# A fourth tile for weight first parts (and, for a while, remainders) in the first mixer, constants fetched one by one, and output tiles stored by another queue

## The chip, the cores and the metric

The kernel runs on one core of a Trainium2 chip. The core has five engines with queues of their own: TensorE (PE, matrix products; its weight loads are listed apart as PEld), VectorE (DVE), ScalarE (ACT), GpSimd (POOL) and SyncE (SP, which here only issues DMAs). Each works through its own list of instructions in order and waits at semaphores for the others. The metric is the time of one execution on the device in microseconds (us), as the median of several runs.

## What is computed

Two layers of a decoder trunk on x of 256 rows (time) by 2048 columns, all in float32. The first layer has a mixer of two parallel halves, the second an attention mixer; each is followed by a gated feed-forward with a causal convolution. Only the first mixer and the very end of the last feed-forward matter here:

```python
def mixer_ab(h, w_in, sp_w, sp_b, v_gain, lower_bound, o_gain, w_out):
    u, v, q, f, i, g = jnp.split(h @ w_in, cuts, axis=-1)        # each 256 x 1024
    u = gelu(u); v = rms_norm(gelu(v) per head) * v_gain
    mixed = einsum('hts,bcshd->bcthd', tril(sp_w), v) + sp_b     # chunks of 128 rows
    y_a = u * mixed
    y_b = hgrn2(q, f, i, g, lower_bound, o_gain)                 # 8 heads, gated recurrence
    return concatenate([y_a, y_b], -1) @ w_out

x = x + mixer_ab(rms_norm(x), ...)
x = x + conv_ffn(rms_norm(x), ...)
x = x + mixer_c(rms_norm(x), ...)
x = x + conv_ffn(rms_norm(x), ...)
```

## The kernel before

x lies transposed on chip: 16 tiles of 128 columns by 256 rows (xT[0] to xT[15]), kept in seven larger tiles of 1, 1, 2, 2, 2, 4 and 4 of them (x0, x1, x2, x4, x6, x8, x12 in the lists of instructions). Every weight is streamed through once, in **pieces** of 128 x 1024 numbers (512 KB): 128 in the first mixer, 816 in the kernel (a few are rounded in two halves).

float32 accuracy comes from two rounded parts. For each piece, SyncE loads `w` (L196), ScalarE rounds it to the first part `wh` (L183), VectorE subtracts to get the remainder `wl` (L184). TensorE then multiplies three times, activations likewise being split: wh with the first part, wl with the first part, wh with the remainder (L357 to L359 in `project_four`, L338 to L340 in `project_tok`, L314 in `project`). The tiles come from `three` (L169): 5 buffers of w, 3 of wh and 3 of wl in the first mixer; the tile of piece n is that of piece n-3, so its rounding must wait until TensorE is through with piece n-3. `weights` (L194) ties the loads, roundings and subtractions to the order of the pieces.

Everything else is fitted between the pieces. Its work is written as Python generators that lie in `queue` and `flight`; `tick()` (L133), called once for each piece, lets each of up to depth[0] generators go on to its next `yield`. A generator thus hands out its instructions some pieces later, and a yield more or less moves what follows by a piece. `held(r, "wl")` puts an instruction behind the last wl handed out, `early` ahead of the one three pieces on, `tied` behind the last matmul. Within these ties a scheduler sets each engine's final order, by its own simulated times and by when buffers come free.

The first mixer's program order: `project_first` for v (w_v), while the norm's sums of squares are made; then `fetch_late` (L536) four times, which issues on ScalarE's queue the loads of the spatial weights `spw` and `spb` into the two tiles `wt`, of the remaining columns of the parameters `pp`, and of the masks `kst`; then, piece by piece, w_f (2 groups of 8 pieces, `gates`), the 8 heads' w_q with w_i between them (`values`, `flip`, `hgrn`), w_g (`gated`), w_u (`spatial`) and the output projection w_abo (`add_four`). Beside the pieces of w_f and the first of w_q runs `mixes` (L581): gelu on v, its sums of squares, the normalisation of gv in four multiplications (L606), and the spatial product (L570, L572). `hgrn(h)` (L686 on) is the recurrence of one head; `gated(j)` multiplies its normalised output (L793) by silu of the gate (L827).

`add_four(q, ...)` (L476) takes a quarter of the output projection (4 column tiles): ScalarE copies it (L478), VectorE transposes it in two halves (L370), 16 transfers of 32 KB by SyncE and GpSimd (L377) set the blocks in place in `dst`, and some pieces later VectorE adds them to x (L490); each x tile is split again for the feed-forward's first matmuls (ScalarE L385, VectorE L389) and its squares are summed (L452, L456). The quarter q=3 is added while the first pieces of the feed-forward's w_up are already under way.

At the end, the last feed-forward adds three quarters of its output in the same manner (`add_y`, L1298), the last quarter tile by tile straight from the sums (L1331), and `finish_x` (L1310) stores each finished tile: the last four tiles (m 12 to 15) one by one (L1314), the others when their larger tile is complete (L1316), all on SyncE.

Of the kernel before, what the change touches and what calls it, by code (L numbers as in the profile page):

```python
# [15 lines left out]
P = 128  # L16
# [39 lines left out]
def tile_trunk(ctx: ExitStack, tc: tile.TileContext, x, pp_d, cst_d, mlev_d, msk_d,  # L56
# [98 lines left out]

    deep = {"pool": None, "turn": 0, "dma": None}

# [11 lines left out]
    def three(n):  # L169
# [10 lines left out]
        return w, wh, wl  # L180

    def halves(w, wh, wl):
        r = deep["wh"] = SC.activation(wh, w, AF.Copy)  # L183
        deep["wl"] = V.tensor_tensor(wl, w, wh.bitcast(F32), ALU.subtract)  # L184
        return r
# [8 lines left out]
    def weights(src, n, rows=None):  # L194
        w, wh, wl = three(n)
        in_order("w", nc.sync.dma_start(w if rows is None else w.rearrange("p (m c) -> p m c", m=rows), src))  # L196
        halves(w, wh, wl)
        for what in ("wh", "wl"):
            in_order(what, deep[what])
        pieces[0] += 1  # L200
        for n_, what, r in list(ahead):
            if n_ <= pieces[0]:
                tc.add_manual_dep(deep[what].ins, r.ins.name, order, reason="before")
                ahead.remove((n_, what, r))
        return wh, wl
# [296 lines left out]
    def mixer_ab(norm):  # L502
# [21 lines left out]
        for g, ps in enumerate(project_first(w_v, norm, lambda: queue.append(finish()))):  # L524
# [5 lines left out]
            else:  # L530
                drain()
                Rt = norm.Rt
                last = ps
        A = norm.a

        def fetch_late(*args, behind="wh"):  # L536
            r = SC.dma_start(*args)
            tc.add_manual_dep(r.ins, deep[behind].ins.name, order, reason="queue order")
# [5 lines left out]

        wt = [wide("wt").rearrange("p (h c) -> p h c", h=NH) for _ in range(2)]
        fetch_late(wt[0], spw_d)
        fetch_late(wt[1], spb_d.partition_broadcast(P))
        fetch_late(pp[:, C_CW:NPP], pp_d[:, C_CW:NPP])
        msk = hp.tile([P, NL * P], U16, tag="msk", name="msk")
        kst = hp.tile([P, NL - 1, 2, P], F32, tag="E", name="kst", bufs=2).rearrange("p a b c -> p (a b c)")[:, 0:NL * P]  # L550
        fetch_late(kst, msk_d)
        near, tri = kst[:, (NL - 1) * P:NL * P], cst[:, K_TRI:K_TRI + P]
# [28 lines left out]
        def mixes():  # L581
# [19 lines left out]
            for g in range(2):  # L601
                yield
                for T in range(2):
                    i = (2 * g + T) * 4
                    v4 = gv[g][:, T].rearrange("p (h d) -> p h d", d=P)
                    held(V.tensor_tensor(v4, v4, ss[:, i:i + 4].unsqueeze(2).to_broadcast([P, 4, P]),  # L606
                                         ALU.mult), "wl")
# [4 lines left out]
            for h in range(0, NH, 2):  # L612
                ps = bank()
                both = [mix(h + i, ps[:, i * S:(i + 1) * S]) for i in range(2)]
                for m in both:
                    next(m)
                for m in both:
                    next(m, None)
                yield


# [7 lines left out]
        def bound():  # L629
# [10 lines left out]
            V.tensor_scalar(lb, lb, 2.0 ** -63, None, ALU.max)  # L640

        queue.append(mixes())
        lf, kq = [], []

# [41 lines left out]
        def hgrn(h):  # L686
# [29 lines left out]
            waiting.append(diagonal)  # L716
            yield
            if waiting:
# [7 lines left out]
            for li in reversed(range(NL)):  # L726
# [12 lines left out]
                if 1 < n < 64:  # L739
                    yield  # L740
            for _ in range(2):
                yield
# [55 lines left out]
        def flip(itok, late):  # L798
            tmp, rows = (hp.tile([P, 512], F32, tag="ar", name=nm(n), bufs=3) for n in ("tmp", "rows"))
            V.transpose(tmp, late)  # L800
            V.transpose(rows.rearrange("p (c j) -> p c j", j=BLK), view(tmp, BLK - 1, (BLK, P // 8), (-1, BLK)))
            yield
            for b in range(4):
                nc.gpsimd.dma_start(itok[BLK * b:BLK * (b + 1), 1], rows[BLK * (3 - b):BLK * (4 - b)])
            yield
            itoks.append((itok, steps[0]))

        def values(j):
            ps = project_tok(w_i[j], norm)
            itok = hp.tile([P, 2, 512], F32, tag="tok", name=nm("itok"), bufs=2)  # L810
            late = hp.tile([P, 512], F32, tag="ar", name=nm("late"), bufs=3)
            SC.activation(cols2(late), of_two(ps[1]), AF.Copy, scale=Rt[:, 1:2])
# [30 lines left out]
        for h in range(NH):  # L843
# [7 lines left out]
            for T in range(2):  # L851
                q = kq[h][:, 2 - T]
                SC.activation(back(q) if T else q, view(ps, T, (2, P)), AF.Copy, scale=omlb[:, h:h + 1])
            queue.append(hgrn(h))
        for j in range(2):
            ps = project_four(w_g[4 * j:4 * j + 4], A, KT)
# [38 lines left out]
        for q in range(4):  # L895
# [12 lines left out]
            if q == 0:  # L908
                depth[0] = 2
            add_four(q, ps, z, tmp, dst, nxt, 2 if q in (1, 2) else 1, (nc.sync, nc.gpsimd) if q else (nc.gpsimd,))  # L910
        es.close()
        banks(ctx, 4)
# [304 lines left out]
    def ffn(l, norm, last):  # L1217
# [69 lines left out]
        def add_y(q, finish):  # L1287
# [5 lines left out]
            def rest():  # L1293
                for _ in range(3 if near else LAG - 2 * (q == 3)):
                    yield
                for i in range(4):
                    m = 4 * q + i
                    held(V.tensor_tensor(xT[m], xT[m], zt[:, i], ALU.add), "wl")  # L1298
                    if finish:
                        finish_x(m)  # L1300
                    if not near and (q < 3 or i % 2):
                        yield
# [7 lines left out]
        def finish_x(m):  # L1310
            if last:
                t, i, end = part[m]
                if m >= KT - 4:
                    nc.sync.dma_start(out[:, m, :], xT[m])  # L1314
                elif m == end:
                    nc.sync.dma_start(out[:, m - i:m + 1, :], t)  # L1316
            else:
                nxt.feed(m)
# [127 lines left out]
```

## Time and profile before

| | us |
|---|---|
| median of 3 runs | 2169.62 (2169.5, 2169.62, 2169.9) |
| the profiled execution | 2170.91 |
| its span, first to last instruction | 2169.1 |
| first mixer within it | 0 to about 387 |
| first feed-forward | about 387 to 1058 |
| second mixer, second feed-forward | about 1058 to 1506, to 2169 |

The spans are from one profiled execution on the one core, with a mean granted TensorE clock of 1.000. Durations in the text are from its trace; a matmul's listed length (0.38 us) is longer than the distance to the next one's start, as matmuls overlap, so distances between starts are what counts. In rows of the trace, `out<-in` are tiles by the program's names, and the bracket at the end gives the time for which the engine sat idle before the instruction and what ended it. The lists of instructions further down come from the compiled programs: they show order, not time.

### The profile page before, as it was taken

What the parts mean: (1) busy time and instruction counts of PE and PEld (TensorE: products, weight loads), DVE (VectorE), ACT (ScalarE), POOL (GpSimd) and SP (SyncE); (2) the same over time, 40 slices, a digit from 0 to 9 for tenths busy, and PEclk for the clock granted to TensorE, in tenths of its full rate; (3) what the DMA queues carried; (4) which work ended last, traced back from release to release, by engine and by line L of the source; (5) the groups of instructions that cost most, each with busy time, mean ns of one, the idle gap of its engine ahead of it and who ended that gap; (6) DMA issues with size and microseconds to landing.
All of it is one profiled execution on the core that took longest, in us unless ns stands there. A gap on an engine that the chain in (4) does not pass through costs nothing.

```text
span 2169.1 us, 32427 instructions
## 1 busy us (share of the span) xinstructions
PE 2162.7 (100%) x10874; PEld 1900.2 (88%) x10874; DVE 1616.6 (75%) x2258; ACT 1322.6 (61%) x1951; POOL 458.9 (21%) x841
## 2 busy tenths in 40 slices
PE   9999999999999999999999999999999999999999
PEld 8898888888888888888888888888888888888888
DVE  7788768777567757876987787877787577667766
ACT  7688756666556546664565556766666466456642
POOL 0242231212012002111133443221211012012102
PEclk9999999999999999999999999999999999999999
DMA  8665777877676767776777767777777677767766
GB/s 307 204 183 183 217 227 229 247 228 231 214 222 206 241 206 221 242 216 208 245 229 226 241 206 212 227 239 222 240 243 214 200 235 218 228 213 225 235 209 189
DMA packets 492871, 484.06 MB, mean 223 GB/s; under 512 B 115264, under 2 KB 460496, under 8 KB 492576
## 3 DMA queue, kind: packets, MB, share of 16 engines
q1 hardware_dynamic: 465888, 453.27, 66.6%
q0 software_dynamic: 25088, 26.44, 5.3%
q10 hardware_dynamic: 1728, 2.28, 0.4%
q8 instruction: 85, 1.39, 0.3%
q14 instruction: 82, 0.67, 0.1%
HBM read 435.18 MB, written 2.11 MB: 202 GB/s over the span
## 4 chain that ended last, share of the span: by engine, by line
PE 96%; DVE 1%; DMA 1%; ACT 1%; issue 0%; SPq 0%; DVEq 0%; ACTq 0%
PE pm L358 26%; PE pm L357 26%; PE pm L359 26%; PE pm L338 5%; PE pm L340 4%; PE pm L339 4%; PE pm L314 3%; DVE wl L184 1%; DMA w<-in_w_f 1%; PE pm L246 0%; ACT wh L183 0%; DMA w<-in_w_v 0%; PE pm L270 0%; PE px L1040 0%; PE px L1094 0%
## 5 line engine op out<-in xcount | busy, mean ns | idle before, releaser
L184 DVE TENSOR_TENSOR wl<-w,wh 128x1024 fp32r<-128x1024 f32 (+1 forms) x820 | 994.7, 1218 | 453.1 <-ACT wh L183 439.2
L183 ACT ACTIVATE wh<-w 128x1024 fp32r<-128x1024 f32 (+1 forms) x820 | 859.2, 1051 | 640.7 <-PE pm L359 492.8
L358 PE MATMUL pm<-wl,a 128*128 128x512 f32 x1728 | 655.2, 379 | 1.0 <-DVE wl L184 0.9
L357 PE MATMUL pm<-wh,a 128*128 128x512 f32 x1728 | 655.9, 380 | 0.0
L359 PE MATMUL pm<-wh,a 128*128 128x512 f32 x1728 | 654.9, 379 | 0.0
L377 POOL DMA_DIRECT2D zt<-tmp x413 | 224.3, 551 | 1134.0 <-DVE tmp L370 1020.8
L358 PEld LDWEIGHTS pm<-wl,a 128*128 128x128 f32 x1728 | 326.6, 189 | 48.0 <-DVE wl L184 2.2
L359 PEld LDWEIGHTS pm<-wh,a 128*128 128x128 f32 x1728 | 326.6, 189 | 46.2
L357 PEld LDWEIGHTS pm<-wh,a 128*128 128x128 f32 x1728 | 326.5, 189 | 46.2
L357 PE MATMUL pm<-wh,hid 128*128 128x512 f32 x688 | 260.8, 379 | 0.0
L358 PE MATMUL pm<-wl,hid 128*128 128x512 f32 x688 | 260.8, 379 | 0.0
L359 PE MATMUL pm<-wh,hid 128*128 128x512 f32 x688 | 260.8, 379 | 0.0
L338 PE MATMUL pm<-wh,a 128*128 128x512 f32 x448 | 170.8, 381 | 0.0
L340 PE MATMUL pm<-wh,a 128*128 128x512 f32 x448 | 169.9, 379 | 0.0
L339 PE MATMUL pm<-wl,a 128*128 128x512 f32 x448 | 169.8, 379 | 0.0
L358 PEld LDWEIGHTS pm<-wl,hid 128*128 128x128 f32 x688 | 130.0, 189 | 18.5
L359 PEld LDWEIGHTS pm<-wh,hid 128*128 128x128 f32 x688 | 130.0, 189 | 18.5
L357 PEld LDWEIGHTS pm<-wh,hid 128*128 128x128 f32 x688 | 130.0, 189 | 18.4
L377 POOL DMA_DIRECT2D turn<-tmp x160 | 87.2, 553 | 226.0 <-DVE tmp L370 128.4
L1252 ACT ACTIVATE conv<-zt,pp 128x256 f32<-128x256 f32 x176 | 103.4, 589 | 46.5 <-DMA zt<-tmp 31.9
L370 DVE STREAM_TRANSPOSE tmp<-z 128x512 f32<-128x512 f32 x120 | 100.9, 858 | 9.3 <-ACT z L1238 6.8
L1253 DVE SCALAR_TENSOR_TENSOR conv<-zt,pp,conv 128x255 f32<-128x255 f32 x176 | 84.1, 478 | 30.7 <-ACT conv L1252 25.8
(244 smaller groups left out, 2202.4 us busy)
## 6 DMA issues: line engine op xcount, KB each, us to landing
w<-in_w_up SPq DMA_DIRECT2D x352, 512.0 KB, 5.1
w<-in_w_dn SPq DMA_DIRECT2D x176, 512.0 KB, 5.0
w<-in_w_cqkv SPq DMA_DIRECT2D x96, 512.0 KB, 5.0
w<-in_w_abo SPq DMA_DIRECT2D x32, 512.0 KB, 5.0
w<-in_w_cg SPq DMA_DIRECT2D x32, 512.0 KB, 5.3
w<-in_w_co SPq DMA_DIRECT2D x32, 512.0 KB, 5.1
zt<-tmp SPq DMA_DIRECT2D x414, 32.0 KB, 2.2
zt<-tmp POOLq DMA_DIRECT2D x413, 32.0 KB, 2.0
```

What stands on the lines that cost most here:

```text
L183: r = deep["wh"] = SC.activation(wh, w, AF.Copy)
L184: deep["wl"] = V.tensor_tensor(wl, w, wh.bitcast(F32), ALU.subtract)
L338: PE.matmul(to_two(ps[T]), ah, h, start=k + i == 0, stop=False)
L339: PE.matmul(to_two(ps[T]), ah, l, start=False, stop=False)
L340: deep["last"] = PE.matmul(to_two(ps[T]), al, h, start=False, stop=k + i == KT - 1)
L357: PE.matmul(to_rows(ps[T]), ah, h, start=not begun and k + i == ks[0], stop=False)
L358: PE.matmul(to_rows(ps[T]), ah, l, start=False, stop=False)
L359: deep["mm"] = deep["last"] = PE.matmul(to_rows(ps[T]), al, h, start=False, stop=not more and k + i == ks[-1] + 1)
L370: V.transpose(tmp.rearrange("p (b m i t) -> p b m i t", b=4, m=4, t=2)[:, :, :, :, T], src(T).rearrange("p (m b j) -> p b m j", m=4, b=4))
L377: queues[(a + b) % len(queues)].dma_start(dst[BLK * b:BLK * (b + 1), :, a * n:(a + 1) * n], tmp[BLK * a:BLK * (a + 1), b * 4 * n:(b + 1) * ...
L1252: held(SC.activation(c, z, AF.Identity, bias=pp[:, cb:cb + 1], scale=w(2)))
L1253: V.scalar_tensor_tensor(c[:, 1:], z[:, :S - 1], w(1), c[:, 1:], ALU.mult, ALU.add)
```

## The change

- In the first mixer the pieces' tiles now come from a function `fourth`. Every fourth piece takes its wh from a further tile ("wh4"), so that four are in use in turn. During the heads every fourth piece also takes its wl from the pool's two "QK" tiles: from the end of `mixes`, when their last users are through, until ahead of w_g, which needs them again.
- Room for this comes from `flip`: its three "ar" tiles become one; its temporary shares the tile "junk", and the rows are written back over `late`.
- The constants are no longer fetched in one go: a generator `constants` issues kst, then spw, then spb, two ticks apart, and the tail of pp is fetched by GpSimd's queue ahead of w_g.
- `mixes` yields ahead of each of gv's four multiplications rather than of each pair. The last head waits one tick longer ahead of its diagonal, and the last two heads one less ahead of their products.
- At the end of the kernel, the second quarter's four additions are no longer a tick apart, and tiles 8 to 11 are stored in two pieces of 256 KB by GpSimd in place of one of 512 KB by SyncE.

```diff
-    deep = {"pool": None, "turn": 0, "dma": None}
+    deep = {"pool": None, "turn": 0, "dma": None, "fourth": {}}
...
+    def fourth(n):
+
+        deep["turn"] += 1
+        w = wp.tile([P, n], F32, tag="w", name=nm("w"), bufs=5)
+        more = deep["fourth"] if deep["turn"] % 4 == 0 else {}
+        return w, *(pool.tile([P, n], F32R, tag=tag, name=nm(what), bufs=bufs) for what in ("wh", "wl")
+                    for pool, tag, bufs in (more.get(what, (wp, what, 3)),))
...
     def weights(src, n, rows=None):
-        w, wh, wl = three(n)
+        w, wh, wl = (fourth if deep["fourth"] else three)(n)
...
         A = norm.a
-
-        def fetch_late(*args, behind="wh"):
-            r = SC.dma_start(*args)
+        deep.update(fourth={"wh": (hp, "wh4", 1)}, turn=0)
+
+        def fetch_late(*args, behind="wh", eng=SC):
+            r = eng.dma_start(*args)
...
-        fetch_late(wt[0], spw_d)
-        fetch_late(wt[1], spb_d.partition_broadcast(P))
-        fetch_late(pp[:, C_CW:NPP], pp_d[:, C_CW:NPP])
...
-        fetch_late(kst, msk_d)
+
+        def constants():
+            for dst, src in ((kst, msk_d), (wt[0], spw_d), (wt[1], spb_d.partition_broadcast(P))):
+                fetch_late(dst, src)
+                yield
+                yield
...
             for g in range(2):
-                yield
                 for T in range(2):
+                    yield
                     i = (2 * g + T) * 4
...
                 for m in both:
                     next(m, None)
                 yield
+            deep["fourth"]["wl"] = (hp, "QK", 2)
...
+        start(constants())
         queue.append(mixes())
...
             waiting.append(diagonal)
-            yield
+            for _ in range(1 + (h == NH - 1)):
+                yield
...
-            for _ in range(2):
+            for _ in range(2 - (h >= NH - 2)):
                 yield
...
-            tmp, rows = (hp.tile([P, 512], F32, tag="ar", name=nm(n), bufs=3) for n in ("tmp", "rows"))
+            tmp, rows = hp.tile([P, 512], F32, tag="junk", name=nm("tmp"), bufs=1), late
...
-            late = hp.tile([P, 512], F32, tag="ar", name=nm("late"), bufs=3)
+            late = hp.tile([P, 512], F32, tag="ar", name=nm("late"), bufs=1)
...
+        fetch_late(pp[:, C_CW:NPP], pp_d[:, C_CW:NPP], eng=nc.gpsimd)
+        deep["fourth"].pop("wl", None)
         for j in range(2):
             ps = project_four(w_g[4 * j:4 * j + 4], A, KT)
...
             add_four(q, ps, z, tmp, dst, nxt, 2 if q in (1, 2) else 1, (nc.sync, nc.gpsimd) if q else (nc.gpsimd,))
+        deep["fourth"] = {}
         es.close()
...
-                    if not near and (q < 3 or i % 2):
+                    if not near and (q < 3 and not (last and q) or i % 2):
                         yield
...
                     nc.sync.dma_start(out[:, m, :], xT[m])
+                elif m >= KT - 8:
+                    if i % 2:
+                        nc.gpsimd.dma_start(out[:, m - 1:m + 1, :], t[:, i - 1:i + 1])
                 elif m == end:
```

The new lines push everything behind them down, so the same source line has a higher number after the change: L184 becomes L192, L606 becomes L618, L793 and L827 become L808 and L842, L490, L389, L456 and L370 become L498, L397, L464 and L378. Tiles carry a running number in the lists.

**VectorE at the second half of w_f**, where gv is normalised. wl_141 is the remainder of that half's first piece. Before:

```order
L184 TENSOR_TENSOR wl_133_719<-w_131_717,wh_132_718 128x1024
L425 SCALAR_TENSOR_TENSOR rt_127_677<-ss_543 128x16
L426 TENSOR_TENSOR rt_127_677<-rt_127_677,rm_126_676 128x16
L427 SCALAR_TENSOR_TENSOR ss_543<-rt_127_677,ss_543 128x16
L606 TENSOR_TENSOR gv_64_405<-gv_64_405,ss_543 128x512 x2
L606 TENSOR_TENSOR gv_85_504<-gv_85_504,ss_543 128x512 x2
L184 TENSOR_TENSOR wl_141_764<-w_139_762,wh_140_763 128x1024
```

After:

```order
L192 TENSOR_TENSOR wl_133_717<-w_131_715,wh_132_716 128x1024
L433 SCALAR_TENSOR_TENSOR rt_127_676<-ss_539 128x16
L650 RECIPROCAL gm_540<-gm_540 128x8
L434 TENSOR_TENSOR rt_127_676<-rt_127_676,rm_126_675 128x16
L192 TENSOR_TENSOR wl_141_761<-w_139_759,wh_140_760 128x1024
L435 SCALAR_TENSOR_TENSOR ss_539<-rt_127_676,ss_539 128x16
L651 TENSOR_TENSOR gm_540<-gm_540 128x8
L652 TENSOR_TENSOR gm_540<-gm_540 128x8
L618 TENSOR_TENSOR gv_64_405<-gv_64_405,ss_539 128x512
L653 TENSOR_SCALAR gm_540<-gm_540 128x8
L618 TENSOR_TENSOR gv_64_405<-gv_64_405,ss_539 128x512
L618 TENSOR_TENSOR gv_85_504<-gv_85_504,ss_539 128x512
```

The remainder has moved ahead of the four multiplications; the next one stands ahead of the last of them.

**VectorE at the first group of w_u**, where the first half of the gate is applied (o is the recurrence's output, gz the gate). Before:

```order
L184 TENSOR_TENSOR wl_426_2906<-w_424_2904,wh_425_2905 128x1024
L422 TENSOR_SCALAR rm_419_2874<-sos_971 128x2x4
L425 SCALAR_TENSOR_TENSOR rt_420_2875<-sos_971 128x2x4
L426 TENSOR_TENSOR rt_420_2875<-rt_420_2875,rm_419_2874 128x2x4
L427 SCALAR_TENSOR_TENSOR sos_971<-rt_420_2875,sos_971 128x8
L790 TENSOR_TENSOR sos_971<-sos_971,Rt_89_514 128x8
L793 TENSOR_TENSOR o_259_1597<-o_259_1597,sos_971 128x512 x2
L827 TENSOR_TENSOR gz_416_2869<-gz_416_2869,o_259_1597 128x512
L370 STREAM_TRANSPOSE tmp_434_2967<-gz_416_2869 128x512
L184 TENSOR_TENSOR wl_429_2927<-w_427_2925,wh_428_2926 128x1024
L827 TENSOR_TENSOR gz_416_2869<-gz_416_2869,o_259_1597 128x512
L184 TENSOR_TENSOR wl_432_2947<-w_430_2945,wh_431_2946 128x1024
```

After:

```order
L192 TENSOR_TENSOR wl_424_2904<-w_422_2902,wh_423_2903 128x1024
L430 TENSOR_SCALAR rm_417_2872<-sos_963 128x2x4
L192 TENSOR_TENSOR wl_427_2925<-w_425_2923,wh_426_2924 128x1024
L433 SCALAR_TENSOR_TENSOR rt_418_2873<-sos_963 128x2x4
L434 TENSOR_TENSOR rt_418_2873<-rt_418_2873,rm_417_2872 128x2x4
L435 SCALAR_TENSOR_TENSOR sos_963<-rt_418_2873,sos_963 128x8
L805 TENSOR_TENSOR sos_963<-sos_963,Rt_89_514 128x8
L808 TENSOR_TENSOR o_258_1595<-o_258_1595,sos_963 128x512 x2
L842 TENSOR_TENSOR gz_414_2867<-gz_414_2867,o_258_1595 128x512 x2
L192 TENSOR_TENSOR wl_430_2945<-w_428_2943,wh_429_2944 128x1024
```

The remainder wl_429 of before (wl_427 after) has moved from behind the first L827 and a transpose to ahead of the whole block, and none stands between the two multiplications any longer.

**VectorE at the end of the output projection**, where the quarter q=2 (x8) is added and q=3 (zo) transposed. Before:

```order
L490 TENSOR_TENSOR x8_75<-x8_75,dst_598_3847 128x256
L184 TENSOR_TENSOR wl_645_4089<-w_643_4087,wh_644_4088 128x1024
L389 SCALAR_TENSOR_TENSOR a_641_4081<-x8_75,pp_77,a_641_4081 128x256
L456 TENSOR_TENSOR acc_490_3291<-acc_490_3291,sq_642_4084 128x256
L490 TENSOR_TENSOR x8_75<-x8_75,dst_598_3847 128x256
L184 TENSOR_TENSOR wl_650_4114<-w_648_4112,wh_649_4113 128x1024
L389 SCALAR_TENSOR_TENSOR a_646_4106<-x8_75,pp_77,a_646_4106 128x256
L370 STREAM_TRANSPOSE tmp_634_4043<-zo_633_4042 128x512
L456 TENSOR_TENSOR acc_490_3291<-acc_490_3291,sq_647_4109 128x256
L370 STREAM_TRANSPOSE tmp_634_4043<-zo_633_4042 128x512
L490 TENSOR_TENSOR x8_75<-x8_75,dst_598_3847 128x256
L184 TENSOR_TENSOR wl_655_4139<-w_653_4137,wh_654_4138 128x1024
```

After:

```order
L498 TENSOR_TENSOR x8_75<-x8_75,dst_596_3845 128x256
L397 SCALAR_TENSOR_TENSOR a_639_4079<-x8_75,pp_77,a_639_4079 128x256
L464 TENSOR_TENSOR acc_488_3289<-acc_488_3289,sq_640_4082 128x256
L192 TENSOR_TENSOR wl_643_4087<-w_641_4085,wh_642_4086 128x1024
L498 TENSOR_TENSOR x8_75<-x8_75,dst_596_3845 128x256
L397 SCALAR_TENSOR_TENSOR a_644_4104<-x8_75,pp_77,a_644_4104 128x256
L464 TENSOR_TENSOR acc_488_3289<-acc_488_3289,sq_645_4107 128x256
L192 TENSOR_TENSOR wl_648_4112<-w_646_4110,wh_647_4111 128x1024
L498 TENSOR_TENSOR x8_75<-x8_75,dst_596_3845 128x256
L378 STREAM_TRANSPOSE tmp_632_4041<-zo_631_4040 128x512
L397 SCALAR_TENSOR_TENSOR a_649_4129<-x8_75,pp_77,a_649_4129 128x256
L464 TENSOR_TENSOR acc_488_3289<-acc_488_3289,sq_650_4132 128x256
```

The remainders stood between an addition and L389; now they stand ahead of the addition, so that L389 follows it at once. The second transpose comes two rows after this piece, behind one more remainder (wl_653). On SyncE, one more weight load stands ahead of each of the last three quarters' groups of transfers.

## The prediction

> **What bounds the kernel now.** I read the page's busy shares first, then the windows by stage (columns: length, then busy time of each engine with its count), then what TensorE waited for.
>
> ```profile
> PE 2162.7 (100%) x10874; PEld 1900.2 (88%) x10874; DVE 1616.6 (75%) x2258; ACT 1322.6 (61%) x1951; POOL 458.9 (21%) x841
> ...
> 0.00:387.00 387.00, 384.69 (x2481) 341.08 (x2482) 298.83 (x467) 274.43 (x518) 90.33 (x167) 1.00 0.72 223
> 387.00:1058.00 671.00, 671.00 (x3110) 587.58 (x3110) 488.63 (x642) 392.27 (x517) 112.99 (x208) 1.00 0.72 221
> ...
> PE pm L358 <- DVE wl L184: 0.9, 2, 0.7
> ```
>
> TensorE is the bound: 2162.7 of the span's 2169.1 us, at a granted clock of 1.00 in both stages shown. In the second stage, the first feed-forward, it is busy for all of 671.00 us: 3110 matmuls, 671.00/3110 = 0.216 us each. That is its pitch when nothing is late. Every matmul of the change's stage is still issued after it, in nearly the same order, so the change cannot touch this pitch. What it can win is the time in which TensorE stood still in the first mixer (0 to 387 us). The waits name two stops on a weight's remainder (wl, written by VectorE at L184), 0.9 us in all. I looked for others in the starts of matmuls, where the distance is more than the pitch, and found a third. The rows of TensorE at the three places (start, length, instruction, in brackets the idle time before it):
>
> ```profile
> 68.58 0.38 PE L357 MATMUL pm<-wh,a 128*128 128x512 f32 x1
> 69.66 0.48 PE L358 MATMUL pm<-wl,a 128*128 128x512 f32 x1 [0.70 <-DVE wl L184]
> 69.98 0.38 PE L359 MATMUL pm<-wh,a 128*128 128x512 f32 x1
> ...
> 240.57 0.38 PE L357 MATMUL pm<-wh,a 128*128 128x512 f32 x1
> 241.01 0.48 PE L358 MATMUL pm<-wl,a 128*128 128x512 f32 x1
> 241.33 0.38 PE L359 MATMUL pm<-wh,a 128*128 128x512 f32 x1
> ...
> 375.58 0.38 PE L357 MATMUL pm<-wh,a 128*128 128x512 f32 x1
> 376.15 0.48 PE L358 MATMUL pm<-wl,a 128*128 128x512 f32 x1 [0.20 <-DVE wl L184]
> 376.47 0.38 PE L359 MATMUL pm<-wh,a 128*128 128x512 f32 x1
> ```
>
> From the start of the first row to that of the third there should be two pitches, 0.43 us. At the first place there are 1.40 (a loss of 0.97), at the second 0.76 (0.33), at the third 0.89 (0.46). The mixer's ceiling of gain is their sum, 1.76 us, or 0.08% of the time: less than the 0.2% (4.3 us) that a measurement of this kernel can tell from no change.
>
> The Trainium skill, page "Perfetto Trace Analysis", section "Identifying the Most-Contended Engine", holds against this reading that a matmul's busy time says little and that the busy share of the weight loads is the good measure. By it the 88% of PEld would leave 12% of the mixer, an estimated 46 us, to a kernel whose weights come earlier. The stage without any stop speaks against it: 587.58/671.00 is 87.6% there as well, so here 88% is what a TensorE that never waits for weights shows. I give that rule the smallest chance below.
>
> **The first stop (68.58): a fourth buffer and a spread normalisation.** Ahead of the late remainder stood, in the queues of VectorE and ScalarE:
>
> ```profile
> 65.97 2.50 DVE L606 TENSOR_TENSOR gv<-gv,ss 128x512 f32<-128x512 f32 x4
> 68.39 1.22 DVE L184 TENSOR_TENSOR wl<-w,wh 128x1024 fp32r<-128x1024 f32 x1
> ...
> 65.52 2.00 ACT L183 ACTIVATE wh<-w 128x1024 fp32r<-128x1024 f32 x2
> ```
>
> The four multiplications of gv (2.50 us) stood in one block in front of the remainder, which ended at 69.61. Afterwards the same remainder stands ahead of all four, and one more piece is rounded between the third and the fourth. So it moves at least 2.50 us forward against a loss of 0.97: the stop goes, **gain 0.97**. What could be late next is the piece that then follows the block in part; the pitch of a piece is 12 matmuls, 2.59 us, and VectorE's extra work per piece there is at most two of these multiplications, 1.25 us, beside 1.22 of the remainder. That fits. The constants' fetches are part of this place. They were issued in one go, from 39.85 to 41.66, next to a weight load (first the issues on ScalarE's queue, then two loads with their size and us to landing):
>
> ```profile
> 39.85 0.33 ACTq L537 DMA_DIRECT2D wt<-in_spw  x1
> 41.20 0.46 ACTq L537 DMA_DIRECT2D kst<-in_msk  x1
> ...
> w<-in_w_f SPq DMA_DIRECT2D x1, 512.0 KB, 11.2
> ...
> w<-in_w_up SPq DMA_DIRECT2D x352, 512.0 KB, 5.1
> ```
>
> That load took 11.2 us beside them, against 5.1 for the median of its kind. TensorE has no gap over 0.2 us between 39 and 68, so five buffers of w hide this already: apart, the fetches gain between 0 and what they take part in at the stop just counted. I take 0 more. They each cost one issue of about 0.4 us on ScalarE's queue, before and after alike, and nothing waits for them within 8 us.
>
> **The second stop (240.57): the first parts and remainders go ahead of the gate.**
>
> ```profile
> 235.78 1.28 ACT L96 ACT_TABLE_LOAD   x1
> 238.18 1.05 ACT L183 ACTIVATE wh<-w 128x1024 fp32r<-128x1024 f32 x1
> ...
> 236.60 1.29 DVE L793 TENSOR_TENSOR o<-o,sos 128x512 f32<-128x512 f32 x2
> 238.31 0.69 DVE L827 TENSOR_TENSOR gz<-gz,o 128x512 f32<-128x512 f32 x1 [0.42 <-ACT gz L100]
> 239.80 1.16 DVE L184 TENSOR_TENSOR wl<-w,wh 128x1024 fp32r<-128x1024 f32 x1
> ```
>
> ScalarE rounded that piece at 238.18, after a table load and three of the gate's activations, and VectorE subtracted at 239.80, behind L793, L827 and a transpose (L370). With a fourth buffer of wh both go ahead of the block, at some 234 to 237: 3 to 5 us sooner for a loss of 0.33. The block itself (L793 to both L827, now without a remainder between them) is 1.29 + 2 x 0.69 plus the waits for ScalarE, about 3.5 us; the next remainder then stands behind it and has by my count 1.2 to 2.2 us to spare. **Gain 0.33.** The remainders have still 3 buffers there, the fourth one being given back ahead of w_g, so this spare time cannot grow.
>
> **The third stop (375.58): additions of the residual.** Here the fourth wh works against the path. The quarter q=2 is added among the remainders (VectorE, in order of time; L490 adds, L389 makes the normalised remainder, L456 sums squares):
>
> ```profile
> 349.88 1.06 ACT L183 ACTIVATE wh<-w 128x1024 fp32r<-128x1024 f32 x1 [1.53 <-PE pm L359]
> ...
> 352.11 0.42 DVE L490 TENSOR_TENSOR x<-x,dst 128x256 f32<-128x256 f32 x1
> 353.23 0.54 DVE L389 SCALAR_TENSOR_TENSOR a<-x,pp,a 128x256 fp32r<-128x256 f32 x1 [0.70 <-ACT a L385]
> 353.68 0.41 DVE L456 TENSOR_TENSOR acc<-acc,sq 128x256 f32<-128x256 f32 x1
> 354.48 1.23 DVE L184 TENSOR_TENSOR wl<-w,wh 128x1024 fp32r<-128x1024 f32 x1 [0.38 <-ACT wh L183]
> ...
> 361.42 0.85 DVE L370 STREAM_TRANSPOSE tmp<-zo 128x512 f32<-128x512 f32 x1
> ...
> 362.30 5.91 SPq L377 DMA_DIRECT2D dst<-tmp  x8
> 2136.01 5.13 SPq L377 DMA_DIRECT2D zt<-tmp  x8
> ...
> 370.75 1.10 DVE L490 TENSOR_TENSOR x<-x,dst 128x256 f32<-128x256 f32 x3 [0.42 <-issue]
> ...
> 374.87 2.36 DVE L184 TENSOR_TENSOR wl<-w,wh 128x1024 fp32r<-128x1024 f32 x2
> ```
>
> Before, in two of the four rounds a remainder stands between L490 and L389 and hides the answer of ScalarE (0.70). Afterwards every round is remainder, L490, L389, L456, with that answer in the open: from 352.11 to 354.09 are 1.98 us, with a remainder of 1.14 (to the next start) about 3.1 us per piece, against 2.59 that TensorE needs. VectorE falls back by some 0.5 us in each of three rounds. The second transpose of q=3 (361.42 to 362.27 before) comes then after one more remainder. Counting on: TensorE gives the first round's buffers back at 349.88, so its remainder ends the sooner, and L490 starts at 351.0; three rounds of 3.1 bring 360.3; L490, the first transpose, L389 and L456 (0.4 + 0.8 + 0.45 + 0.4, ScalarE's answer hidden by the transpose) 362.3; the remainder that now stands ahead 363.4, and the second transpose ends at 364.2, **1.9 us later**. SyncE's 8 transfers start at that end (362.30), and the three additions (370.75) start when the last has landed. Then come three round trips and one more addition, and only then the remainder that is late at 375.58 (374.87). So this whole chain shifts. The 8 issues took 5.91 us, 0.8 more than the 5.13 of the later group; without that delay the shift is 1.06, with it 1.86. No reason lets the chain gain here, except that VectorE does the rounds without these delays; then the stop of 0.46 stays or goes. I take the middle, a **loss of 1.46**.
>
> Between ScalarE's activations nothing else moves that TensorE waits for. During the heads (80 to 230) a fourth wl gives VectorE room, but there is no stop there to remove, and the order of the two last heads moves by one piece: gain 0. Should a new stop appear there, its size is of the same kind, 0.1 to 1 us.
>
> **The tail.** The last output row is added when TensorE ends, then two stores are issued:
>
> ```profile
> 2162.07 2.09 DVE L1298 TENSOR_TENSOR x<-x,zt 128x256 f32<-128x256 f32 x6
> ...
> 2165.01 0.42 DVE L1331 TENSOR_TENSOR x<-x,pm 128x256 f32<-128x256 f32 x1 [0.51 <-PE pm L314]
> ...
> 2164.61 1.21 SPq L1314 DMA_DIRECT2D out<-x  x2
> ...
> DMA to landing us min/median/max: 2.0/2.1/2.6
> ...
> zt<-tmp POOLq DMA_DIRECT2D x413, 32.0 KB, 2.0
> ```
>
> The last issue stands at 2165.43 and lands 2.1 us after it; the addition before it is bound by TensorE, so earlier additions gain only the 0.1 us by which the last issue lags. Of the six additions in a row the first two go ahead of the last rows; the four of q=2 (2.09/6 = 0.35 us each) then end at 2162.77 and 2163.47, two by two; the two 256 KB stores, now on GpSimd, start then. Their price from this queue is not in the trace: from below 2.0 us, as its 32 KB transfers, from above twice the longest of L1314's 128 KB, 5.2 us, which ends at 2168.7, 1.1 after the last row's store. I take it nearest to 2.0. **Gain 0.1**, bounds 0.1 won and 1.1 lost.
>
> The Trainium skill ("DMA: Bandwidth & Descriptors", "Issuing engine by pattern") says that simple stores belong on the Sync queue, since GpSimd's is generally slower; by its fit in "Anatomy of one DMA" a 256 KB store would take 2.6 us by estimate. Either way it lands before the last row's store, and the sum stays.
>
> **Sum.** -0.97 - 0.33 + 1.46 - 0.1 = +0.06 us. The profiled execution took 2170.91 us around its span of 2169.1; it is 1.29 above the median of 2169.62. Its 2170.91 becomes 2170.97, and the same step on the median gives **2169.7 us**.
>
> **Rivals.**
> A. All three stops go, and the additions don't fall back: VectorE's 75% leaves room, and 3 rounds of 0.5 us are less than the 2.6 us of a spare buffer. 2169.62 - 1.76 - 0.1 = 2167.8. Against it: the chain of transposes and transfers is not covered by any buffer.
> B. Slower: the 512 KB weight load that now stands one place further ahead of the quarter's 8 transfers on SyncE shares the DMA engines with them. Their landing then takes longer by a third of such a load's 5.1 us, 1.7, on top of the full 1.86: -1.3 - 0.1 + 3.56 = +2.16, so 2171.8. It decides if that load is still under way when the second transpose ends, that is if it starts after 359 us.
> C. The change does not do what it says: remainders still have three buffers where the stops are, each wl waits as before, and the time stays within 0.3 of 2169.6.
> D. The weight loads' 12% are room after all: faster by more than 4.3 us, 2165 or less.
>
> **Chances.** Forecast (2169.3 to 2170.1 by the bounds of its third stop, some tenths more by small waits) 0.50; A 0.25; B 0.12; C 0.08; D 0.02; the rest, a new stop or a late store that adds over 4.3 us, 0.03. C lies in the forecast's own range, so that holds 0.58; to leave out no more than 0.2 the range must take in A and B with some room for their sizes: **2167.4 to 2171.9**. Within 0.2% are forecast, A, B and C: 0.95. Faster by more 0.02, slower by more 0.03.
>
> **What would show it.** Right: at 68.6 and 240.6 matmuls 0.216 us apart; at about 374 a stop of 1.5 to 2.3 us on wl, with the second transpose of q=3 ending some 1.8 us later against TensorE's matmuls than before; the last store issued 0.4 us after TensorE's end. Wrong: no stop at the third place (A), or SyncE's 8 transfers landing more than 3 us after the last issue (B); any new stop in the heads between 80 and 230; or the two stores on GpSimd landing after those of the last rows. The forecast fails as a whole if TensorE's pitch in the mixer is other than 0.216.

## The result and the profile after

| | before | after |
|---|---|---|
| median of 14 runs, us | 2169.85 (2169.1 to 2171.05) | 2174.32 (2173.33 to 2175.28) |
| profiled execution, us | 2170.91 | 2174.30 |
| its span, us | 2169.1 | 2172.5 |
| ratio, 95% interval | | 1.002 [1.0012, 1.0029] |

The change costs 4.47 us, 0.2% of the time. The interval of the ratio lies clear of no change, and the time lies well outside the forecast range.

The first mixer does about what was forecast. What TensorE waited for after the change (engine, line, for whom: us in total, times, longest):

```profile
PE pm L366 <- DVE wl L192: 1.4, 1, 1.4
...
PE pm L322 <- DVE wl L192: 0.3, 1, 0.3
```

The first is in the mixer, the second in the last output tile of the program. TensorE's matmuls at the first:

```profile
373.41 0.38 PE L365 MATMUL pm<-wh,a 128*128 128x512 f32 x1
375.18 0.48 PE L366 MATMUL pm<-wl,a 128*128 128x512 f32 x1 [1.39 <-DVE wl L192]
375.50 0.38 PE L367 MATMUL pm<-wh,a 128*128 128x512 f32 x1
```

Of the three stops on a remainder only the third is left in the mixer. From 373.41 to 375.50 are 2.09 us instead of 0.43: a loss of 1.66, against 0.46 before. So in these two profiles the mixer's stops sum to 1.66 where they were 1.76, and that can't be the 4.47.

The time lies at the end of the program, behind all the work. The chain that ended last is, in both profiles, TensorE's last tile and VectorE's addition of it. After the change (start, us, what):

```profile
2162.17 2.74 PE pm L322 x22
2164.91 0.02 issue
2164.93 0.42 DVE x L1352
```

That addition ends at 2165.35, before the change at 2165.43; but the span goes on for 3.7 us behind it before and for 7.2 after. Neither the chain nor the busy times name what fills these. The instructions of the program's last source line do: it stands for the closing sequence of all engines. First before, then after (duration in ns: shortest, median, longest; starts of the first and the last):

```profile
L1442 POOLq DRAIN  x3: 40/102/7795, 2158.3 to 2168.9; - x3
L1442 SPq DRAIN  x3: 7/7/7, 2168.0 to 2168.3; - x3
```

```profile
L1463 POOLq EVENT_SEMAPHORE  x4: 17/17/17, 2171.8 to 2172.4; - x4
L1463 POOLq DRAIN  x3: 46/102/7850, 2163.9 to 2172.2; - x3
L1463 SPq DRAIN  x3: 7/7/7, 2167.2 to 2172.0; - x3
```

GpSimd closes with a **drain of 7.8 us** (an instruction of the closing sequence, not of the kernel's own work) that begins with its last instruction, or up to 0.5 us ahead of it. Before, it began at 2158.3, among the last of its transfers, and was over at 2166.1, hidden behind SyncE, which waits for the last store until 2168.0. After, GpSimd's last instruction is the second store of tiles 8 to 11:

```profile
2163.09 0.57 POOL L1335 DMA_DIRECT2D out<-x  x1 [4.56 <-DVE x L1316]
...
2163.91 0.56 POOL L1335 DMA_DIRECT2D out<-x  x1 [0.26 <-DVE x L1352]
```

and by its line:

```profile
DMA to landing us min/median/max: 2.5/2.6/2.7
```

The drain then lasts until 2163.9 + 7.85 = 2171.7, and the last exchange of semaphores between the engines starts behind it, at 2171.8. SyncE was through at 2167.2. With the closing of before (2168.0 to 2169.1, 1.1 us) the span would have ended at 2168.3 instead of 2172.5, so in this profile the drain costs **4.2 us**. The stores themselves are not late: they land 2.5 to 2.7 us after their issue, at 2166.6 at the latest. The Trainium skill's fit for such a store ("DMA: Bandwidth & Descriptors", "Anatomy of one DMA") gave an estimate of 2.6 us, and this trace agrees (2.6). The fit doesn't cover what the engine that issued the store still has to do.

### The profile page after: what moved, and what is told of

Its sections match the earlier page's. It is cut to its first block, busy times and chain, and to the rows that moved or that the text cites. A ratio compares the mean times of both kernels' runs of the same rounds, so it can differ in the third digit from the quotient of the medians.

```text
span 2172.5 us, 32466 instructions
## 1 busy us (share of the span) xinstructions
PE 2161.6 (99%) x10874; PEld 1900.3 (87%) x10874; DVE 1615.2 (74%) x2258; ACT 1320.0 (61%) x1951; POOL 459.2 (21%) x844
## 4 chain that ended last, share of the span: by engine, by line
PE 95%; DVE 2%; SPq 1%; DMA 1%; ACT 0%; issue 0%; DVEq 0%; POOL 0%
PE pm L365 26%; PE pm L366 25%; PE pm L367 25%; PE pm L346 4%; PE pm L348 4%; PE pm L347 4%; PE pm L322 2%; PE pm L254 1%; SPq L385 1%; DVE wl L192 1%; PE pm L278 0%; DVE tmp L378 0%; PE px L1058 0%; PE px L1112 0%; DMA zt<-tmp 0%
## 5 line engine op out<-in xcount | busy, mean ns | idle before, releaser
L192 DVE TENSOR_TENSOR wl<-w,wh 128x1024 fp32r<-128x1024 f32 (+1 forms) x820 | 994.5, 1219 | 435.1 <-ACT wh L191 398.3
L378 DVE STREAM_TRANSPOSE tmp<-z 128x512 f32<-128x512 f32 x120 | 100.8, 856 | 9.2 <-ACT z L1256 6.8
```

Of the source, the lines that this page charges most:

```text
L378: V.transpose(tmp.rearrange("p (b m i t) -> p b m i t", b=4, m=4, t=2)[:, :, :, :, T], src(T).rearrange("p (m b j) -> p b m j", m=4, b=4))
```

## The experiments

The theory: GpSimd's drain takes 7.4 to 8 us from its last instruction, and decides the end as soon as that instruction stands later than about 8 us ahead of SyncE's end. Rivals: the mixer's third stop and the new order; stores of 256 KB that are late at the end whoever issues them; a price for bytes or number of stores on GpSimd. A second question is the third stop: whether the fourth wh makes it grow by the way that the prediction gives. Where an experiment is timed against before, the runs of before beside it had medians of 2169.94 to 2170.01.

**a_sync: the changed kernel, with its two stores on SyncE.**

```diff
                 elif m >= KT - 8:
                     if i % 2:
-                        nc.gpsimd.dma_start(out[:, m - 1:m + 1, :], t[:, i - 1:i + 1])
+                        nc.sync.dma_start(out[:, m - 1:m + 1, :], t[:, i - 1:i + 1])
```

> The changed kernel, with tiles 8 to 11 stored by SyncE instead of GpSimd, everything else as changed. Theory (closing drain): after the change GpSimd's last DMA issue stands at 2163.9, its closing drain takes 7.85 us from there and the closing exchange of semaphores 0.8 more; SyncE was through at 2167.2. With GpSimd's last issue back at some 2159 its drain ends at 2166.5 to 2167, before SyncE's part: span 2168.3 to 2168.8, time 4 us below the changed kernel, 2170.0 to 2170.6. Rival 1 (the mixer's new stop and the order of the tail cost it): within 0.5 of the changed kernel, 2174. Rival 2 (stores of 256 KB in the last microseconds are late on any queue): 2172 to 2174, with a landing on SyncE after 2169.

Measured: 2170.50 us (11 runs), ratio to before 1.0003 [0.9994, 1.0012], span 2168.6. GpSimd's drain began at 2158.1 and took as long as before:

```profile
L1463 POOLq DRAIN  x3: 46/171/7940, 2158.1 to 2168.4; - x3
L1463 SPq DRAIN  x3: 7/7/7, 2167.4 to 2168.0; - x3
```

The two stores by their line:

```profile
L1335 SPq DMA_DIRECT2D out<-x x2: 332/332/333, 2162.8 to 2163.4; - x2
...
DMA to landing us min/median/max: 2.0/2.1/2.1
```

So the same two stores, issued by another engine some 0.3 to 0.5 us sooner, cost 3.8 us less. On SyncE they landed 0.5 us faster than on GpSimd (2.1 and 2.6), but either way ahead of the last row's store. Rivals 1 and 2 fall: all else of the change is still there, and SyncE has both stores done by 2167.4.

**b_tail: the kernel before, with the tail of the change alone.**

```diff
-                    if not near and (q < 3 or i % 2):
+                    if not near and (q < 3 and not (last and q) or i % 2):
...
+                elif m >= KT - 8:
+                    if i % 2:
+                        nc.gpsimd.dma_start(out[:, m - 1:m + 1, :], t[:, i - 1:i + 1])
```

> The kernel before, with only the tail of the change (second quarter's additions without ticks, tiles 8 to 11 as two stores of 256 KB on GpSimd). Theory (closing drain): GpSimd's last issue at 2163.5 to 2164, so the span ends 8.6 us later, 2172.1 to 2172.6, and the time is 3.4 to 4.4 above before. Rival (the mixer costs the time): within 0.3 of before.

Measured: 2173.49 us (10 runs), ratio 1.0016 [1.0007, 1.0025], span 2172.1; 3.5 us above before, with nothing of the mixer changed. Of the change's 4.47 us, 3.5 thus come with the tail alone, and a_sync's 0.5 with the rest (by itself not to be told from no change); the two add up to 4.0, and the missing 0.5 is less than runs of one kernel differ by.

```profile
L1445 POOLq DRAIN  x3: 46/102/7395, 2163.9 to 2171.8; - x3
L1445 SPq DRAIN  x3: 7/7/7, 2167.7 to 2171.5; - x3
```

**b_m13, b_m14, b_m15: the kernel before, with a single store of 128 KB on GpSimd**, that of tile 13, 14 or 15 (shown for tile 14).

```diff
                 if m >= KT - 4:
-                    nc.sync.dma_start(out[:, m, :], xT[m])
+                    (nc.gpsimd if m == 14 else nc.sync).dma_start(out[:, m, :], xT[m])
```

> The kernel before, with the store of tile 13 (128 KB) on GpSimd. Theory: GpSimd's closing drain starts with its last DMA issue and takes 7.4 to 7.95 us; SyncE is through at about 2167.5 to 2168. Tile 13 is issued at about 2160, so the drain ends at 2167.5 to 2168: right at the point from which it decides. Time within 0.7 of before. Rival (any store on GpSimd after its transfers costs, or it costs by count): 3 us or more above before.

> The kernel before, with one store of 128 KB, of tile 14, on GpSimd instead of SyncE. Theory: what counts is when GpSimd issues last, not bytes or count: issue at about 2164.55, drain of 7.8, end at 2173.2, time about 4 above before. Rival (256 KB are too large for this queue at the end): one store of 128 KB lands 2 to 3 us after its issue, before the last row's, and the time stays within 0.5 of before.

> The kernel before, with the store of tile 15, the last, on GpSimd. Theory: issue at 2165.5, end 8.6 later, 2174; that is 0.5 to 1 above the same with tile 14 (2174.34), as the issue is 0.5 to 0.9 later: 2174.8 to 2175.4. Rival (a fixed price for a late store on GpSimd): as with tile 14, or less, since then nothing is left for SyncE to wait for.

Measured: 2170.04 (ratio 1.0002 [0.9992, 1.0012]), 2174.34 (1.0019 [1.0009, 1.0029]) and 2175.74 us (1.0027 [1.0016, 1.0037]). One store of the same size and kind costs nothing, 4.4 or 5.7 us, by nothing but its place in time. Tile 15's time is 0.3 above the 2174.8 to 2175.4 expected; as its interval overlaps tile 14's, that it costs more than tile 14 is only probable. The closing rows of the three, GpSimd's drain and SyncE's for tile 13, and GpSimd's for 14 and 15:

```profile
L1442 POOLq DRAIN  x3: 40/171/7615, 2159.1 to 2167.8; - x3
L1442 SPq DRAIN  x3: 7/7/7, 2166.9 to 2167.5; - x3
```

```profile
L1442 POOLq DRAIN  x3: 40/171/7613, 2165.0 to 2173.5; - x3
```

```profile
L1442 POOLq DRAIN  x3: 40/172/7613, 2164.7 to 2173.1; - x3
```

With tile 13 the drain ends at 2166.7, 0.2 us ahead of SyncE (2166.9): this is about the point from which it decides. (Between the profiles of 14 and 15 TensorE's own end differs by 1.2 us, as executions of one kernel do; the 15th addition is the last in both.)

**b_copy: a copy in place of a store.** GpSimd's DMAs stay as before; after tile 14's addition it copies that tile over tile 0, which is stored by then. Nothing is left out.

```diff
                     nc.sync.dma_start(out[:, m, :], xT[m])
+                    if m == 14:
+                        nc.gpsimd.tensor_copy(xT[0], xT[m])
```

> The kernel before, and a copy on GpSimd of tile 14 (128 x 256) into tile 0, which is stored by then, as GpSimd's last instruction, at about 2164.5; no DMA of GpSimd is moved. Theory A (the long drain follows whatever GpSimd did last): the end moves by 4 us or more, as with the store of tile 14. Theory B (it belongs to DMAs that GpSimd has issued, and counts from the last of them): the drain starts after the copy but is over by 2167 at the latest, and the time stays within 0.5 of before.

Measured: 2173.83 us (ratio 1.0017 [1.0007, 1.0027]), 3.8 above before.

```profile
2163.50 0.40 POOL L1316 COPY x<-x 128x256 f32<-128x256 f32 x1 [5.39 <-DVE x L1333]
```

```profile
L1444 POOLq DRAIN  x3: 40/167/7375, 2163.5 to 2171.7; - x3
```

Theory A holds, though the time rose by slightly less than its 4 us, and B falls. The drain isn't work left over from DMAs: GpSimd had been idle for 5.4 us since issuing the last of them, and with a copy of 0.40 us as its last instruction the drain still took 7.4 us.

**b_none: GpSimd out of the last group of transfers.** Its 16 transfers go to SyncE and ScalarE.

```diff
-                       (nc.sync, nc.gpsimd, SC) if near else (nc.sync, nc.gpsimd))
+                       (nc.sync, SC) if near else (nc.sync, nc.gpsimd))
```

> The kernel before, with the last group of 16 transfers shared by SyncE and ScalarE alone; GpSimd's last work is then some 6 us earlier, at 2150. Theory (the drain is a fixed 7.4 to 8.1 us after GpSimd's last instruction): it starts at about 2150 and is over by 2158, and again costs nothing. Rival (it waits for something at the end of the program, such as the other engines or outstanding stores): it ends no earlier than in before, 2166. The time itself rises by 0.5 to 2, as the last weight's first part waits for eight issues of ScalarE and its remainder stands behind tile 14's addition.

Measured: 2170.34 us (ratio 1.0003 [0.9993, 1.0013]).

```profile
L1442 POOLq DRAIN  x3: 40/102/7578, 2148.0 to 2167.9; - x3
```

The drain began at 2148.0 and was over at 2155.5, long before any other engine was through: it waits neither for them nor for their stores. What fills its 7.6 us within GpSimd, no run shows. The time rose by 0.4, less than the 0.5 to 2 expected, and can't be told from no change.

**a_sync_three: a_sync, with three buffers again from the output projection on.**

```diff
+        deep["fourth"] = {}
         nxt = Norm(C_FFN, turn=True)
...
-        deep["fourth"] = {}
         es.close()
```

> As a_sync, and the fourth tile given up ahead of the output projection (three buffers of each there, as before the change). Theory (the fourth first part lets VectorE's additions follow each other without a remainder between, and shifts the second transpose of q=3): the stop near 374 falls from 1.66 us back to about 0.46, and TensorE ends some 1.2 us sooner than in a_sync: time 0.6 to 1.2 below a_sync. Rival (the stop grew because a weight load stands ahead of the quarter's transfers, or because TensorE comes there 1.3 us sooner): the stop stays at 1.3 to 1.7.

Measured: 2169.41 us (11 runs), ratio 0.9999 [0.9991, 1.0008]; 1.1 below a_sync, as expected, though the intervals of the two overlap. The profile is clearer. The stop, expected back at about 0.46, is gone: the waits name only TensorE's start and one on the last tile, and the matmuls at the place follow each other at the pitch.

```profile
PE warm L150 <- DVE ones L86: 1.1, 1, 1.1
PE pm L322 <- DVE wl L192: 0.4, 1, 0.4
```

```profile
373.94 0.38 PE L365 MATMUL pm<-wh,a 128*128 128x512 f32 x1
374.16 0.38 PE L366 MATMUL pm<-wl,a 128*128 128x512 f32 x1
374.37 0.38 PE L367 MATMUL pm<-wh,a 128*128 128x512 f32 x1
```

How the stop grows is seen where q=3 is transposed and added (VectorE and SyncE). First the changed kernel, then a_sync_three:

```profile
360.94 0.83 DVE L378 STREAM_TRANSPOSE tmp<-zo 128x512 f32<-128x512 f32 x1
...
361.80 6.21 SPq L385 DMA_DIRECT2D dst<-tmp  x8
...
369.91 1.09 DVE L498 TENSOR_TENSOR x<-x,dst 128x256 f32<-128x256 f32 x3 [1.71 <-DMA dst<-tmp]
...
373.91 1.22 DVE L192 TENSOR_TENSOR wl<-w,wh 128x1024 fp32r<-128x1024 f32 x1
```

```profile
359.76 0.84 DVE L378 STREAM_TRANSPOSE tmp<-zo 128x512 f32<-128x512 f32 x1
...
360.64 5.58 SPq L385 DMA_DIRECT2D dst<-tmp  x8
...
368.60 1.09 DVE L498 TENSOR_TENSOR x<-x,dst 128x256 f32<-128x256 f32 x3
...
372.63 2.36 DVE L192 TENSOR_TENSOR wl<-w,wh 128x1024 fp32r<-128x1024 f32 x2
```

And b_tail, whose mixer is that of before, with TensorE at the same place:

```profile
360.93 0.85 DVE L370 STREAM_TRANSPOSE tmp<-zo 128x512 f32<-128x512 f32 x1
...
369.75 1.09 DVE L490 TENSOR_TENSOR x<-x,dst 128x256 f32<-128x256 f32 x3
...
373.79 2.36 DVE L184 TENSOR_TENSOR wl<-w,wh 128x1024 fp32r<-128x1024 f32 x2
...
375.08 0.38 PE L357 MATMUL pm<-wh,a 128*128 128x512 f32 x1
375.30 0.38 PE L358 MATMUL pm<-wl,a 128*128 128x512 f32 x1
375.52 0.38 PE L359 MATMUL pm<-wh,a 128*128 128x512 f32 x1
```

Against the last matmul before the place of the stop (in us):

| | before | b_tail | a_sync_three | after |
|---|---|---|---|---|
| that matmul starts at | 375.58 | 375.08 | 373.94 | 373.41 |
| second transpose ends ahead of it by | 13.3 | 13.3 | 13.3 | 11.6 |
| from there to the first addition | 8.5 | 8.0 | 8.0 | 8.1 |
| remainder starts ahead of it by | 0.7 | 1.3 | 1.3 | -0.5 |
| stop | 0.46 | 0 | 0 | 1.66 |

With the fourth tile the second transpose is 1.7 us later against TensorE, and the remainder 1.8 us later than in a_sync_three and b_tail. The stop of 0.46 in the profile of before is that execution's: SyncE's transfers landed a median of 4.4 us after their issue there, 3.1 to 3.4 in the other three, and none of the six other profiles with the mixer of before (b_tail to b_none) has a stop here. The two profiles with the fourth tile in the output projection (after, a_sync) both have 1.66.

The rival of a TensorE that comes sooner falls: it is 1.6 us sooner in a_sync_three too, without a stop. The rival of the weight load ahead of the transfers isn't told apart by this run, which takes that load back as well, but the rows leave little for it: the load was issued at 361.1, yet from the transpose's end to the first addition it took 8.1 us instead of 8.0, and the shift of the transpose stands ahead of any transfer.

**best2 and best3: the last group shared otherwise.** Both are a_sync_three with another list of queues for the last 16 transfers: SyncE and GpSimd alone (best2), or 4, 8 and 4 for SyncE, GpSimd and ScalarE (best3). First best2, then best3:

```diff
-                       (nc.sync, nc.gpsimd, SC) if near else (nc.sync, nc.gpsimd))
+                       (nc.sync, nc.gpsimd) if near else (nc.sync, nc.gpsimd))
...
-                       (nc.sync, nc.gpsimd, SC) if near else (nc.sync, nc.gpsimd))
+                       (nc.sync, nc.gpsimd, SC, nc.gpsimd) if near else (nc.sync, nc.gpsimd))
```

> As a_sync_three, and the last group of transfers by SyncE and GpSimd alone, without ScalarE, so that the last weight's first part isn't queued behind five issues (4.2 us). Theory: TensorE's stop of 0.4 in the last tile goes; GpSimd's last issue moves to about 2158.5, so its drain ends at 2166.3, about when SyncE is through: time 0.2 to 0.6 below a_sync_three. Rival: the additions of tiles 8 to 11 come later (SyncE has 8 issues in place of 5), their stores go ahead of the last row's, and the end stays or is 0.5 later.

> As a_sync_three, with the last group of 16 transfers shared 4 SyncE, 8 GpSimd, 4 ScalarE instead of 6, 5, 5. Theory: ScalarE is free one issue (0.84 us) sooner for the last weight's first part, so TensorE's stop of 0.55 there goes or shrinks; GpSimd's last issue moves by three issues of 0.54, to 2158, and its drain ends at 2166.0, still ahead of SyncE: time 0.2 to 0.5 below a_sync_three (2169.41). Rival: the drain becomes the end, as in best2 (2169.75): the same or 0.3 to 0.6 above a_sync_three.

Measured: 2169.75 (ratio 0.9997 [0.9988, 1.0006]) and 2169.42 us (0.9997 [0.9988, 1.0006]), so neither is better than a_sync_three, as the rivals had it. In best2's profile TensorE's stop at the last tile is gone, but GpSimd's drain begins only at 2160.3, not 2158.5, and ends at 2168.4, 0.7 behind SyncE. In best3's it begins at 2160.4 and ends with SyncE, and TensorE's stop at the last tile is 0.8 us, not smaller than the 0.4 of a_sync_three. The rows of best2:

```profile
L1463 POOLq DRAIN  x3: 46/102/8103, 2160.3 to 2168.9; - x3
L1463 SPq DRAIN  x3: 7/7/7, 2167.7 to 2168.7; - x3
```

a_sync_three is 0.6 us below the kernel before, and that can't be told from no change; none of these versions beats it measurably.

## Why the prediction was wrong

- **First stop, gain 0.97.** The changed kernel doesn't have it, nor have the four experiments built on it. But its size was one execution's: of the six other profiles with the mixer of before, two (b_m13, b_none) have no stop here, the other four 0.20 to 0.55.
- **Second stop, gain 0.33.** Right: all seven profiles with the mixer of before have it, none of the five with the changed one.
- **The heads, gain 0.** Here 0.36 us were won: from the program's 1401st matmul to the 1601st (188.0 to 207.5 us before) the five profiles of the changed mixer take 0.36 less than all seven of the other. Which wait went isn't shown.
- **Third stop, loss 1.06 to 1.86, taken 1.46.** The mechanism was right: VectorE's rounds took 3.05 to 3.09 us (3.1 forecast), the second transpose came 1.7 later against TensorE (1.9 forecast) and the remainder 1.8 (1.86 at most forecast; the working gives 364.2 - 362.27 = 1.93). The stop grew by 1.20 over the profile of before and by 1.66 over the usual 0. With three buffers there it is gone (a_sync_three). That the order of VectorE is the way it comes about is read from its rows; a_sync_three by itself only shows that the fourth tile there is needed for it.
- **Mixer in sum.** By the profile of before, -0.97 - 0.33 - 0.36 + 1.20 = -0.46, where the forecast's terms gave +0.16. By the six others the mixer loses 0.4 to 1.0 (1.66 - 0.36 - 0.33, less 0 to 0.55). a_sync's 0.5 above before fits the latter, but its interval takes in no change.
- **The tail, gain 0.1, bounds 0.1 won and 1.1 lost.** This is the step that failed. It priced the two stores on GpSimd by when they would land ("from below 2.0 us ... from above ... 5.2 us"), and the landing was near its lower bound, 2.5 to 2.7 us; the sign that was to show it wrong, stores landing after those of the last rows, did not come (2166.6 against 2167.2). But it took the landing of the last store for the end of the program. Another thing has to end too, GpSimd's drain, which counts from its last instruction and not from a store's landing: 2163.9 + 7.85 instead of 2158.3 + 7.8. The cover was SyncE's end at 2168.0, so about 1.9 us of delay were free, and the drain went 5.6 later; by a_sync this costs 3.8 us. The row is in the trace of before, under the last source line, and the forecast doesn't use it.
- **The rivals.** A (no third stop), C (no effect) and D (faster by over 4.3) fall with the stop of 1.66 and the time. B's 2171.8 is nearest, but not for its reason: its condition was met, as the load was issued at 361.1, and the transfers were slower by 0.1 us, not 1.7. The Trainium skill's rule that simple stores belong on the Sync queue ("DMA: Bandwidth & Descriptors", "Issuing engine by pattern") pointed the right way, and was set aside in the forecast because the stores would land in time. They did. The rule's reason, that GpSimd's queue is generally slower, holds here too (2.6 us against 2.1), but that half microsecond isn't where the 3.8 us lie.
- **The range.** It held 2167.4 to 2171.9, the time is 2174.32. A late store that adds over 4.3 us had a share of the last 0.03, without a working; the 4.47 came about otherwise, as the stores weren't late.

## What to carry to other kernels

The end of a program is a race of all engines' closing sequences, not the landing of the last store: list each engine's last instruction and what it still does behind it (the rows of the program's last source line show it), and give none of its late work to the engine whose closing is longest. A queue that is idle at the end isn't free for that reason; here GpSimd must have its last instruction some 8 us ahead of the others' end. A stop that one profile shows may be that execution's own: read the same place in other profiles before giving its removal a price. And a fourth buffer for one of two paired operands changes the order of the engine that makes the other, so look for the round trips that its instructions had been hiding.

## What the runs showed of the hardware

GpSimd's closing drain took 7.4 to 8.1 us in all twelve profiles, and was over 6.5 to 7.4 us after the end of its last instruction: after transfers of 32 KB, stores of 128 and 256 KB, and a copy without any DMA, and whether SyncE was through 12 us after the drain's end (b_none) or 5 us ahead of it (tile 15). In the same sequence SyncE's drain took 0.007 us, and the longest of the others 1.1 (ScalarE), 2.2 (TensorE) and 0.5 to 1.5 us (VectorE). In the profiles of before and after, the chain of waits and the busy times don't show GpSimd's, since a drain isn't counted as work.
